# The second layer's modulation, from TensorE matmuls to sums over k tiles on VectorE

## The chip, the cores and the metric

One core of a Trainium2 chip runs the program. The metric is device time in microseconds (us) of one execution; the runs of the kernel before give a median of 1842.97 us (three runs, 1840.48 to 1843.57).

The engines are TensorE (PE in the profile; its weight loads are PEld), VectorE (DVE), ScalarE (ACT), GpSimd (POOL) and SyncE (SP), whose queue issues the DMAs.

## What is computed

The reference is a two-layer diffusion trunk over 512 latent and 256 context tokens of width 1024. Each layer scales and shifts its normed input by a modulation that depends on the conditioning vector alone:

```python
for l in range(DEPTH):                       # DEPTH = 2
    mod_l = (jax.nn.silu(c) @ ada_w[l] + ada_b[l])[:, None, :]     # ada_w[l]: 1024 x 6144
    mod_c = jax.nn.silu(c_ctx) @ ada_w[l] + ada_b[l]
    sh1, sc1, g1, sh2, sc2, g2 = jnp.split(mod_l, 6, axis=-1)
    csh1, csc1, cg1, csh2, csc2, cg2 = jnp.split(mod_c, 6, axis=-1)
    h_l = _rms(x, norm_w[l, 0]) * (1 + sc1) + sh1
    h_c = _rms(xc, norm_w[l, 0]) * (1 + csc1) + csh1
    ...
    x = x + g1 * (y_l @ w_o[l])
    x = x + g2 * _mlp(_rms(x, norm_w[l, 1]) * (1 + sc2) + sh2, mlp_w1[l], mlp_w2[l])
```

The MLP is `square(relu(h @ w1)) @ w2` with a hidden width of 4096. In the second layer the context is needed only as far as keys and values go, so of its modulation only the first third (shift and scale of the mixer's norm) is used.

## The kernel before

**Layout.** Features lie on the 128 partitions, tokens along the free dimension. A weight matrix is cut into chunks of 128 output columns; one chunk holds eight k tiles of 128x128. `linear` takes one chunk through PSUM: for the context's 256 columns and then for the latent's 512, eight k tiles by three passes (the numbers are split into a high and a low part, high x high, high x low, low x high), 24 matmuls each, into one bank, and then calls an evacuation. The tag `mm` has two banks, which alternate between context and latent.

**Weights.** `weight` loads a chunk in two pieces of 128x512 (tile `wst`, three buffers, L234), ScalarE casts the high part (`whi`, L250), GpSimd subtracts to get the low part (`wlo`, L251); six buffers each.

**The MLP** of the first layer (`mlp`) has four blocks b = 0..3; in each, eight up chunks and eight down chunks. The evacuation of an up chunk is a chain: ScalarE's relu into `tmp` (L1224), VectorE's product with PSUM (L1225), ScalarE's cast (L340), VectorE's subtraction (L341). That of a down chunk is one VectorE instruction that adds into the residual (L1240). The first three up chunks of b = 0 run together (`linears`), k tile by k tile, their matmuls at L289; all others run at L272.

**The modulation of the second layer** runs in the background of this MLP. It is a generator, `ada(rnd)` for rnd = 3, 4, 5, each for a third of the 6144 columns. For each of eight k tiles it loads two weight tiles of 128x1024 floats (tag `ast`, five buffers, L508), yields, and then has four matmuls (L512): the stationary operand is the 128x32 tile `cc[:, k]`, which holds the two conditioning vectors (latent, context) in its first two columns, the moving operand 512 columns of the weights, and each of the four writes another strip of 32 partitions of the bank `ad`, over the eight k tiles. Then `ada_out` transposes the bank on VectorE (L470) and adds the bias.

**Order.** `run` adds up the cost that each linear yields (its columns over 2400, 2.56 units for context and 5.12 for latent) and for each `pace` units takes one step of the background generator. Steps so stand in program order behind the evacuation of some linear. The program's engines get their instructions from a scheduler that simulates the program and prefers earlier ones in program order among those it thinks ready. Before block b = 3 what is left of the generator is run to its end.

```python
def tick(self, cost):
    self.clock += cost
    while self.clock >= self.pace:
        self.clock -= self.pace
        next(self.background, None)
```

Of the kernel before, what the change touches and what calls it, by code (L numbers as in the profile page):

```python
# [12 lines left out]
F32 = mybir.dt.float32  # L13
# [4 lines left out]
ALU = mybir.AluOpType  # L18
AX = mybir.AxisListType

P = 128
D = 1024
KT = 8
# [15 lines left out]

PACE = math.inf, 4.0
RATIO0, RATIO1, RATIO2 = 1.1, 1.6, 1.2
FILL0, FILL1 = 12, 6
NLAST, NFIRST = (2, 3), (3, 2)
# [10 lines left out]
def chain(*gens):  # L56
    for g in gens:
        yield from g
# [35 lines left out]
class Kernel:  # L94
    def __init__(self, ctx, tc, a):
# [8 lines left out]
        self.n, self.side = 0, 1  # L104
        self.clock, self.pace, self.background = 0.0, PACE[0], iter(())

# [59 lines left out]
    def mix(self, main, fill, ratio):  # L166

        done = [0.0, 0.0]
        gens = [iter(main), iter(fill)]
        while gens[0] is not None or gens[1] is not None:  # L170
            i = 0 if gens[1] is None or (gens[0] is not None and done[0] * ratio <= done[1]) else 1
            c = self.step(gens[i], i)
            if c is None:
                gens[i] = None
            else:
                done[i] += c
                yield c

    def weave(self, main, fill, ratio):
        self.run(self.mix(main, fill, ratio))  # L180
# [21 lines left out]
    def load(self, name, shape, dt=F32):  # L202
        t = self.cp.tile(list(shape), dt, tag=name, name=name)
        self.nc.sync.dma_start(t, self.a[name])
        return t

    def constants(self):
        nc, cp = self.nc, self.cp
        self.cmod = self.load("cmod", (P, 2, KT))
        self.ident = cp.tile([P, P], F32, tag="ident", name="ident")  # L210
        make_identity(nc, self.ident)
        self.ones = cp.tile([P, 32], F32, tag="ones", name="ones")
        nc.vector.memset(self.ones, 1.0)
        self.half = cp.tile([P, 32], F32, tag="half", name="half")
        nc.vector.memset(self.half, 0.0)
        nc.vector.memset(self.half[0:64, 0:16], 1.0)
        nc.vector.memset(self.half[64:128, 16:32], 1.0)
        self.adab = self.load("ada_b", (P, 2, 48))
        self.normw = self.load("norm_w", (P, 2, 2, KT))

# [242 lines left out]
        self.mod = [self.cp.tile([P, 48, 2], F32, tag=f"mod{l}", name=f"mod{l}") for l in range(2)]  # L463
        self.A = [[self.cp.tile([P, KT, 2], F32, tag=f"A{l}{n}", name=f"A{l}{n}") for n in range(2)] for l in range(2)]

    def ada_out(self, l, firsts, n, o):

        nc = self.nc
        tr = self.tmp()[:, :32 * n * len(firsts)]
        nc.vector.transpose(tr, o)  # L470
        for i, t0 in enumerate(firsts):
            mod = self.mod[l][:, t0:t0 + n, :]
            nc.vector.tensor_tensor(mod, tr[:, 32 * n * i:32 * n * (i + 1)].rearrange("p (t r) -> p t r", r=32)[:, :, 0:2],
                                    self.adab[:, l, t0:t0 + n].unsqueeze(2).to_broadcast([P, n, 2]), op=ALU.add)
            for m, first in enumerate((8, 32)):
                a, b = max(t0, first), min(t0 + n, first + 8)
                if a < b:
                    nc.vector.scalar_tensor_tensor(self.A[l][m][:, a - first:b - first, :], mod[:, a - t0:b - t0, :], 1.0,
                                                   self.normw[:, l, m, a - first:b - first].unsqueeze(2)
                                                   .to_broadcast([P, b - a, 2]), op0=ALU.add, op1=ALU.mult)  # L480
# [17 lines left out]
                yield 0.6  # L498
        self.ada_out(0, (2 * c, 8 + 2 * c), 2, o)

    def ada(self, rnd):

        nc = self.nc
        o = self.ps("ad")
        for k in range(KT):
            ws = [self.pieces() for _ in range(2)]
            for j, w in enumerate(ws):
                nc.sync.dma_start(w.rearrange("p a b -> p (a b)"), self.a["ada_w"][rnd - 1, k, j])  # L508
            yield 0.0
            for g in range(4):  # L510
                c = 32 * g
                nc.tensor.matmul(o[c:c + 32, :], lhsT=self.cc[:, k, :], rhs=ws[g // 2][:, g % 2, :], start=(k == 0),  # L512
                                 stop=(k == KT - 1), tile_position=(0, c))
            yield 1.0
        self.ada_out(rnd // 3, (rnd % 3 * 16,), 16, o)

    def ada_near(self):

# [750 lines left out]
    def main(self, out):  # L1269
        nc, a = self.nc, self.a  # L1270
# [4 lines left out]
        w = self.rows_weight(a["w_hv"])  # L1275
# [6 lines left out]
        acc = {}  # L1282
# [3 lines left out]
        r, f = self.norm_sums(acc, BOTH)  # L1286
# [71 lines left out]
        bc = self.proj_last(0, y2, x, BOTH)  # L1358
        first = self.mlp_first(0)
        h, ready = self.norm(x, self.A[0][1], self.mod[0][:, 24:32, :], bc)  # L1360
        self.clock, self.background, self.pace = 0.0, chain(*[self.ada(r) for r in range(3, 6)]), PACE[1]
        bc = self.mlp(0, h, x, BOTH, first, ready)

        w = self.rows_weight(a["w_dv"])
# [169 lines left out]
```

## Time and profile before

| | |
|---|---|
| median of three runs | 1842.97 us (1840.48 to 1843.57) |
| profiled execution | 1845.22 us, its span 1843.4 us |
| TensorE busy | 1765.9 us, 96% of the span |
| VectorE busy | 866.9 us, 47% |
| ScalarE busy | 756.3 us, 41% |
| GpSimd busy | 542.8 us, 29% |
| mean granted clock of TensorE | 0.991 of full |

The profile is one execution, recorded instruction by instruction. A row of a timeline gives the start from the beginning of the span, the duration (of several merged instructions from the first's start to the last's end), the engine, the line of the kernel, the operation, its output and inputs by their names in the program, their shapes and how many instructions are merged. In square brackets stands how long the engine was idle before, and what ended that. Matmuls are pipelined and overlap in the record, so the distance between two starts is what one costs, not its duration. A busy share is an average over stages; what bounds a stage is read from that stage.

### The profile page before, as it was taken

The page shows a single profiled execution, that of the slowest core. Times are in us where ns is not written, and L with a number is a line of the kernel's source. Part 1 is how long each engine was busy: PE and PEld are TensorE (multiplying, and loading weights), DVE is VectorE, ACT ScalarE, POOL GpSimd, SP SyncE. Part 2 cuts the span into 40 slices and gives each one's busy share as a digit, 9 for nine tenths or more (in the row PEclk, how much of TensorE's full clock was granted, in tenths as well). Part 3 has the DMA queues.
Part 4 walks back from the last instruction along what each step waited for, and adds up shares of the span by engine and source line. Part 5 has one row for each costly group of instructions (what it writes and reads, how often), then busy time and mean ns, then how long its engine had stood idle before and what let it go on. Part 6 is the DMA issues. An engine that isn't in the chain of part 4 may idle for free. (4 is left out here: it accounts for less than half of the span.)

```text
span 1843.4 us, 28900 instructions
## 1 busy us (share of the span) xinstructions
PE 1765.9 (96%) x11404; PEld 1447.1 (79%) x11404; DVE 866.9 (47%) x1964; ACT 756.3 (41%) x1510; POOL 542.8 (29%) x440
## 2 busy tenths in 40 slices
PE   5999999999999999999999999998998989999999
PEld 4877867787888877788888887776775878888887
DVE  5456766578555212211212237888769651212121
ACT  3554554466434212312312324566756343323241
POOL 0322323101122222223232321322233334444442
PEclk9999999999999999999999999999999989999999
DMA  8442241102133454412112131211121223233232
GB/s 304 139 137 77 98 150 42 38 24 98 46 103 133 154 171 165 141 60 64 63 63 63 63 98 63 67 41 35 41 88 57 75 69 97 97 98 97 97 98 92
DMA packets 81112, 170.94 MB, mean 93 GB/s; under 512 B 9424, under 2 KB 13008, under 8 KB 80976
## 3 DMA queue, kind: packets, MB, share of 16 engines
q1 hardware_dynamic: 80976, 169.09, 27.8%
q8 instruction: 89, 1.46, 0.3%
q14 instruction: 47, 0.39, 0.1%
HBM read 164.87 MB, written 4.19 MB: 92 GB/s over the span
## 5 line engine op out<-in xcount | busy, mean ns | idle before, releaser
L272 PE MATMUL mm<-lat,whi 128*128 128x512 f32 (+1 forms) x2908 | 908.8, 392 | 3.1 <-ACT tmpc L893 1.7
L251 POOL TENSOR_TENSOR wlo<-wst,whi 128x512 fp32r<-128x512 f32 (+1 forms) x374 | 484.9, 1298 | 1162.3 <-ACT whi L250 1080.7
L272 PEld LDWEIGHTS mm<-lat,whi 128*128 128x128 f32 x2908 | 535.2, 188 | 114.8 <-DVE tmpc L1225 5.1
L272 PE MATMUL mm<-lat,wlo 128*128 128x512 f32 (+1 forms) x1454 | 566.7, 390 | 0.0
L250 ACT CAST whi<-wst 128x512 fp32r<-128x512 f32 (+2 forms) x400 | 246.3, 618 | 686.1 <-PE mm L272 596.2
L272 PEld LDWEIGHTS mm<-lat,wlo 128*128 128x128 f32 x1454 | 273.6, 188 | 55.6 <-issue 0.4
L272 PE MATMUL mm<-ctx,whi 128*128 128x256 f32 x1604 | 306.3, 288 | 0.0
L272 PEld LDWEIGHTS mm<-ctx,whi 128*128 128x128 f32 x1604 | 256.6, 192 | 28.3 <-issue 13.7
L272 PE MATMUL mm<-ctx,wlo 128*128 128x256 f32 x802 | 229.0, 285 | 0.0
L1240 DVE SCALAR_TENSOR_TENSOR lat<-mm,mod,lat 128x512 f32<-128x512 f32 x64 | 48.0, 751 | 285.0 <-PE mm L272 285.0
L1225 DVE TENSOR_TENSOR tmp<-mm,tmp 128x512 f32<-128x512 f32 x61 | 42.1, 691 | 256.8 <-ACT tmp L1224 256.8
L272 PEld LDWEIGHTS mm<-ctx,wlo 128*128 128x128 f32 x802 | 154.2, 192 | 1.5 <-issue 1.0
L341 DVE TENSOR_TENSOR lat<-tmp,lat 128x512 fp32r<-128x512 f32 (+1 forms) x74 | 51.6, 700 | 41.0 <-ACT lat L340 40.7
L340 ACT CAST lat<-tmp 128x512 fp32r<-128x512 f32 (+1 forms) x74 | 45.8, 621 | 50.6 <-DVE tmp L1225 45.8
L817 PE MATMUL pv<-ast,lat 128*128 128x256 f32 x312 | 60.5, 302 | 2.4 <-ACT ast L340 1.7
L817 PEld LDWEIGHTS pv<-ast,lat 128*128 128x128 f32 x312 | 44.9, 189 | 12.0 <-ACT ast L340 8.7
L770 PE MATMUL sc<-lat,lat 128*128 128x512 f32 x144 | 45.9, 421 | 3.5 <-ACT p L788 2.4
L788 ACT ACTIVATE p<-ad,sm,sc 128x256 f32<-128x256 f32 x56 | 31.6, 564 | 30.2 <-DVE sm L781 30.0
L1240 DVE SCALAR_TENSOR_TENSOR ctx<-mm,mod,ctx 128x256 f32<-128x256 f32 x32 | 15.5, 483 | 58.8 <-PE mm L272 58.8
L340 ACT CAST ast<-tr 128x512 fp32r<-128x512 f32 x52 | 30.6, 589 | 28.8 <-PE tr L804 28.8
L341 DVE TENSOR_TENSOR ast<-tr,ast 128x512 fp32r<-128x512 f32 x52 | 35.6, 685 | 9.8 <-ACT ast L340 9.3
L804 PE MATMUL tr<-ident,p 128*128 128x128 f32 x208 | 33.7, 276 | 4.2 <-DVE p L1049 2.0
(399 smaller groups left out, 2105.5 us busy)
## 6 DMA issues: line engine op xcount, KB each, us to landing
wst<-in_mlp_w_dram SPq DMA_DIRECT2D x256, 256.0 KB, 2.6
ast<-in_ada_w_dram SPq DMA_DIRECT2D x83, 512.0 KB, 4.5
wst<-in_w_in_dram SPq DMA_DIRECT2D x76, 256.0 KB, 2.7
wst<-in_w_o_dram SPq DMA_DIRECT2D x32, 256.0 KB, 2.6
lat<-in_ada_w_dram SPq DMA_DIRECT2D x13, 512.0 KB, 9.0
lat<-in_x_dram SPq DMA_DIRECT2D x8, 512.0 KB, 6.3
ctx<-in_ctx_dram SPq DMA_DIRECT2D x8, 256.0 KB, 4.5
wst<-in_w_hv_dram SPq DMA_DIRECT2D x8, 256.0 KB, 8.5
```

The costliest lines, as they stand in the source:

```text
L250: nc.scalar.copy(hi[:, :w], st)
L251: (nc.gpsimd if n == P else nc.vector).tensor_sub(lo[:, :w], st, hi[:, :w].bitcast(F32))
L272: self.nc.tensor.matmul(o, lhsT=w(wp, k), rhs=xs[k].at(xp, s), start=(k == 0 and j == 0), stop=(k == nk - 1 and j == 2))
L340: self.nc.scalar.copy(hi, src)
L341: self.nc.vector.tensor_sub(lo, src, hi.bitcast(F32))
L770: nc.tensor.matmul(tiles[j][s], lhsT=l(qi, s), rhs=r(s), start=(i == 0), stop=(i == n - 1))
L788: nc.scalar.activation(p[j][s], tiles[j][s], AF.Exp, bias=neg[:, j:j + 1], scale=sc[:, j:j + 1], accum_out=sm[:, b, j:j + 1])
L804: self.nc.tensor.transpose(o[:, (2 * k + j) * P:(2 * k + j + 1) * P], p[j][s][:, (g + k) * P:(g + k + 1) * P], self.ident)
L817: self.nc.tensor.matmul(o, lhsT=v(x, k), rhs=pt[k][z], start=(k == 0 and j == 0), stop=(k == nk - 1 and j == 2))
L1225: nc.vector.tensor_mul(r, z, r)
L1240: nc.vector.scalar_tensor_tensor(x[m].at(s), z, self.mod[l][:, 40 + m, MOD[s]], x[m].at(s), op0=ALU.mult, op1=ALU.add)
```

## The change

`ada(rnd)` goes. A new generator, `ada_sums`, does the same three rounds on VectorE. A k tile's weights are multiplied by a column of `cc` (one vector's values for that k tile, one per partition) and added into accumulators of 128x512 floats, four for each vector (tag `p`). The first round does both vectors, the other two the latent's alone. What is left is a sum over partitions, for which four matmuls per vector with a constant stationary tile, `pick` (ones in column r), write the four strips of the bank `ad` as before; `ada_out` then runs as before.

The weight tiles are loaded one at a time, two ahead of their use. A step of the generator is one weight tile for one vector, two VectorE instructions. Five steps with loads alone come first; empty steps stand between the last sum, the matmuls and the transpose. The pace goes from 4.0 to 4.5 units a step. `keep_in_program_order` ties an instruction behind the one that the program wrote last on the same engine: an order of issue, without a semaphore.

```diff
--- before.py
+++ after.py
@@ -39,7 +39,7 @@
 
 
 
-PACE = math.inf, 4.0
+PACE = math.inf, 4.5
 RATIO0, RATIO1, RATIO2 = 1.1, 1.6, 1.2
 FILL0, FILL1 = 12, 6
 NLAST, NFIRST = (2, 3), (3, 2)
@@ -215,6 +215,11 @@
         nc.vector.memset(self.half, 0.0)
         nc.vector.memset(self.half[0:64, 0:16], 1.0)
         nc.vector.memset(self.half[64:128, 16:32], 1.0)
+
+        self.pick = cp.tile([P, 2, 32], F32, tag="pick", name="pick")
+        nc.vector.memset(self.pick, 0.0)
+        for r in range(2):
+            nc.vector.memset(self.pick[:, r, r:r + 1], 1.0)
         self.adab = self.load("ada_b", (P, 2, 48))
         self.normw = self.load("norm_w", (P, 2, 2, KT))
 
@@ -463,11 +468,11 @@
         self.mod = [self.cp.tile([P, 48, 2], F32, tag=f"mod{l}", name=f"mod{l}") for l in range(2)]
         self.A = [[self.cp.tile([P, KT, 2], F32, tag=f"A{l}{n}", name=f"A{l}{n}") for n in range(2)] for l in range(2)]
 
-    def ada_out(self, l, firsts, n, o):
+    def ada_out(self, l, firsts, n, o, pin=lambda ins: ins):
 
         nc = self.nc
         tr = self.tmp()[:, :32 * n * len(firsts)]
-        nc.vector.transpose(tr, o)
+        pin(nc.vector.transpose(tr, o))
         for i, t0 in enumerate(firsts):
             mod = self.mod[l][:, t0:t0 + n, :]
             nc.vector.tensor_tensor(mod, tr[:, 32 * n * i:32 * n * (i + 1)].rearrange("p (t r) -> p t r", r=32)[:, :, 0:2],
@@ -498,21 +503,51 @@
                 yield 0.6
         self.ada_out(0, (2 * c, 8 + 2 * c), 2, o)
 
-    def ada(self, rnd):
-
-        nc = self.nc
-        o = self.ps("ad")
-        for k in range(KT):
-            ws = [self.pieces() for _ in range(2)]
-            for j, w in enumerate(ws):
-                nc.sync.dma_start(w.rearrange("p a b -> p (a b)"), self.a["ada_w"][rnd - 1, k, j])
+    def ada_sums(self):
+
+
+
+        nc, pin = self.nc, self.tc.keep_in_program_order
+        src = [(rnd, k, j) for rnd in range(3, 6) for k in range(KT) for j in range(2)]
+        tiles = []
+
+        def load():
+            if src:
+                rnd, k, j = src.pop(0)
+                tiles.append(self.pieces())
+                nc.sync.dma_start(tiles[-1].rearrange("p a b -> p (a b)"), self.a["ada_w"][rnd - 1, k, j])
+
+        for n in range(5):
+            if n < 2:
+                load()
             yield 0.0
-            for g in range(4):
-                c = 32 * g
-                nc.tensor.matmul(o[c:c + 32, :], lhsT=self.cc[:, k, :], rhs=ws[g // 2][:, g % 2, :], start=(k == 0),
-                                 stop=(k == KT - 1), tile_position=(0, c))
-            yield 1.0
-        self.ada_out(rnd // 3, (rnd % 3 * 16,), 16, o)
+        for rnd in range(3, 6):
+            vecs = range(2 if rnd == 3 else 1)
+            acc = [[self.ptile() for _ in range(4)] for _ in vecs]
+            for k in range(KT):
+                for j in range(2):
+                    load()
+                    w = tiles.pop(0)
+                    for r in vecs:
+                        c = self.cc[:, k, r:r + 1]
+                        for g in range(2):
+                            t = acc[r][2 * j + g]
+                            if k == 0:
+                                pin(nc.vector.tensor_scalar(t, w[:, g, :], c, None, op0=ALU.mult))
+                            else:
+                                pin(nc.vector.scalar_tensor_tensor(t, w[:, g, :], c, t, op0=ALU.mult, op1=ALU.add))
+                        yield 0.0
+            yield 0.0
+            o = self.ps("ad")
+            for r in vecs:
+                for g in range(4):
+                    pin(nc.tensor.matmul(o[32 * g:32 * g + 32, :], lhsT=self.pick[:, r, :], rhs=acc[r][g], start=(r == 0),
+                                         stop=(r == len(vecs) - 1), tile_position=(0, 32 * g)))
+            del acc
+            yield 0.0
+            yield 0.0
+            self.ada_out(1, (rnd % 3 * 16,), 16, o, pin)
+            yield 0.0
 
     def ada_near(self):
 
@@ -1358,7 +1393,7 @@
         bc = self.proj_last(0, y2, x, BOTH)
         first = self.mlp_first(0)
         h, ready = self.norm(x, self.A[0][1], self.mod[0][:, 24:32, :], bc)
-        self.clock, self.background, self.pace = 0.0, chain(*[self.ada(r) for r in range(3, 6)]), PACE[1]
+        self.clock, self.background, self.pace = 0.0, self.ada_sums(), PACE[1]
         bc = self.mlp(0, h, x, BOTH, first, ready)
 
         w = self.rows_weight(a["w_dv"])
```

## Rows read from the trace of the kernel before

**Rows 1.** The page's busy times: us, share of the span, instructions, by engine

```profile
PE 1765.9 (96%) x11404; PEld 1447.1 (79%) x11404; DVE 866.9 (47%) x1964; ACT 756.3 (41%) x1510; POOL 542.8 (29%) x440
```

**Rows 2.** Busy us by stretch: PE, PEld, DVE, ACT, POOL; clock, DMA share, GB/s

```profile
574.00:800.00 226.00, 226.00 (x1326) 177.47 (x1325) 48.95 (x87) 58.12 (x107) 62.60 (x49) 1.00 0.47 158
...
800.00:1000.00 200.00, 200.00 (x1153) 177.01 (x1152) 38.14 (x66) 48.15 (x87) 61.95 (x49) 1.00 0.20 64
```

**Rows 3.** TensorE's groups of instructions by line, 560 to 810 us: busy, mean

```profile
L512 PE MATMUL ad<-ast,cc 128*32 128x512 f32 x192 | 25.8, 604 | 0.0
```

**Rows 4.** Timeline of TensorE between linears, 628 to 807 us: start, us, instruction

```profile
628.20 0.39 PE L272 MATMUL mm<-lat,wlo 128*128 128x512 f32 x1
628.42 0.40 PE L272 MATMUL mm<-ctx,whi 128*128 128x256 f32 x2
...
631.29 0.63 PE L272 MATMUL mm<-lat,whi 128*128 128x512 f32 x2
...
637.85 0.51 PE L272 MATMUL mm<-ctx,whi 128*128 128x256 f32 x2
...
647.38 0.51 PE L272 MATMUL mm<-ctx,whi 128*128 128x256 f32 x2
...
712.80 0.39 PE L272 MATMUL mm<-lat,wlo 128*128 128x512 f32 x1
...
798.84 0.40 PE L272 MATMUL mm<-ctx,whi 128*128 128x256 f32 x2
...
807.18 0.40 PE L272 MATMUL mm<-ctx,whi 128*128 128x256 f32 x2
```

**Rows 5.** Timeline behind the opening linear, 577 to 584 us: PE, PEld, DVE, POOL

```profile
577.98 0.39 PE L289 MATMUL sc<-lat,wlo 128*128 128x512 f32 x1
...
580.15 0.51 PE L272 MATMUL mm<-ctx,whi 128*128 128x256 f32 x2
...
583.64 0.14 PEld L512 LDWEIGHTS ad<-ast,cc 128*32 128x32 f32 x4 [0.27 <-DMA ast<-in_ada_w_dram]
...
577.97 1.29 DVE L1225 TENSOR_TENSOR tmp<-mm,tmp 128x512 f32<-128x512 f32 x2 [3.76 <-ACT tmp L1224]
...
579.48 1.96 DVE L341 TENSOR_TENSOR lat<-tmp,lat 128x512 fp32r<-128x512 f32 x2 [0.23 <-ACT lat L340]
...
581.05 1.55 POOL L251 TENSOR_TENSOR wlo<-wst,whi 128x512 fp32r<-128x512 f32 x1 [0.76 <-ACT whi L250]
```

**Rows 6.** Instructions of three VectorE lines: duration ns min/median/max, first and last start

```profile
L421 DVE SCALAR_TENSOR_TENSOR tmp<-lat,A,tmp x8: 742/744/747, 27.1 to 57.1; 128x512 f32<-128x512 f32 x8
...
L423 DVE SCALAR_TENSOR_TENSOR lat<-tmp,mod,lat x24: 737/744/1779, 28.8 to 1136.6; 128x512 fp32r<-128x512 f32 x24
...
L619 DVE TENSOR_SCALAR lat<-lat,oml x8: 474/475/480, 77.9 to 235.2; 128x512 f32<-128x512 f32 x8
```

**Rows 7.** Timeline of VectorE, a down evacuation and an up weight's two chains

```profile
646.50 0.75 DVE L1240 SCALAR_TENSOR_TENSOR lat<-mm,mod,lat 128x512 f32<-128x512 f32 x1 [4.98 <-PE mm L272]
...
708.18 0.43 DVE L1225 TENSOR_TENSOR tmpc<-mm,tmpc 128x256 f32<-128x256 f32 x1 [3.73 <-ACT tmpc L1224]
709.08 0.42 DVE L341 TENSOR_TENSOR ctx<-tmpc,ctx 128x256 fp32r<-128x256 f32 x1 [0.47 <-ACT ctx L340]
714.19 0.69 DVE L1225 TENSOR_TENSOR tmp<-mm,tmp 128x512 f32<-128x512 f32 x1 [4.69 <-ACT tmp L1224]
...
715.57 0.69 DVE L341 TENSOR_TENSOR lat<-tmp,lat 128x512 fp32r<-128x512 f32 x1
```

**Rows 8.** SP's queue, 647 to 665 us; the page's DMA issues (median to landing)

```profile
647.48 0.80 SPq L508 DMA_DIRECT2D ast<-in_ada_w_dram  x2
...
657.91 7.09 SPq L234 DMA_DIRECT2D wst<-in_mlp_w_dram  x2
...
ast<-in_ada_w_dram SPq DMA_DIRECT2D x83, 512.0 KB, 4.5
```

**Rows 9.** Timeline of VectorE in the opening

```profile
2.58 0.25 DVE L462 TENSOR_TENSOR cc<-cmod,sm 128x8 f32<-128x8 f32 x2 [1.23 <-ACT sm L458]
```

## The prediction

> **What bounds the kernel now.** I read the page's busy shares first: TensorE is busy for 1765.9 us of a span of 1843.4, VectorE for 866.9 [rows 1]. An average says nothing of one stage, so the next view is the table by stretch. From 574 to 800 us, where the first layer's MLP runs together with the modulation of the second layer, TensorE is busy in 226.00 of 226 us; from 800 to 1000 us, where no modulation is left, in 200.00 of 200 [rows 2]. VectorE is busy for 48.95 us in the first stretch, a fifth of it [rows 2]. So in this stage the end is set by what stands in TensorE's queue, and the matmuls of L512 stand in it: 192 records, whose time not shared with others is 25.8 us by the groups of lines [rows 3]. The loop issues 96 matmuls there, so each is two records, and the timeline shows them in 24 groups of four matmuls, eight records.
>
> **What the removed matmuls cost.** The timeline of TensorE gives the price as the distance between starts. A weight's two linears, context and latent, take 9.53 us with a group behind them (637.85 to 647.38) and 8.34 without (798.84 to 807.18): 1.19 us a group [rows 4]. I price 21 groups so, 25.0 us. The other three are at the start. Two stand together behind the opening three-weight linear: 577.98 to 580.15, less the 0.22 that lies between linears without a group (628.20 to 628.42), 1.95 us [rows 4, 5]. One waited 0.27 us for its second tile [rows 5]: 1.46. Sum removed: 28.4 us, all of it on the path, since TensorE does not idle.
>
> **What is added on TensorE.** Sixteen matmuls of the same shape (32 columns, 512 wide, 4-byte): eight in a row for the first of the three rounds, which sums for two vectors, four for each of the other two. By the prices above 1.95 + 1.19 + 1.19 = 4.3 us. They wait for VectorE's sums, but the generator leaves an empty step between the last sum and them. There are 5 + 36 + 20 + 20 = 81 steps, one for every 4.5 units of cost, and the three blocks hold 48 weights of 7.68 units, 368.64; counted out, each set of matmuls comes at least one whole linear behind the one after which its last sum stands. So I cost the wait at nothing; its cover is that linear, 2.87 us or more (628.42 to 631.29 [rows 4]).
>
> **What was hidden under the removed groups.** At 578 us the latent outputs of the opening linear end nearly together, and the next linear needs the first of their banks. VectorE's two products run from 577.97 for 1.29 us, so the first bank is free at about 578.6 and the second at 579.3 [rows 5]. The two groups covered that. Without them TensorE could go on at 578.20 and stands until about 578.7: I give back 0.5 us (0 if the bank is free earlier, 1.1 if the second one counts). The rest of VectorE's backlog there meets none of the new sums, since the generator's first five steps hold loads alone and use up the opening linear's ticks.
>
> **What is added on VectorE.** 128 instructions over 128x512 floats: 16 products with a column, and 112 products with a sum in place. Nearest rows: a product with a column, SBUF to SBUF, 475 ns at the median; a product and product with both tensors in SBUF, 744; another such line 737 to 1779 [rows 6]. That is 16 x 0.475 + 112 x 0.744 = 91 us; the upper end, with 1.78 for all of the 112, is 207, the lower 90. I take 744, the row of the same operands and shape, and keep 1.78 for a rival.
>
> Where it lies: a step holds two instructions (1.5 us); a weight has 7.68 / 4.5 = 1.71 steps, 2.54 us in 8.34. In the up half of a block the context chain takes VectorE 1.32 us (708.18 to 709.50) and the latent one 2.07 (714.19 to 716.26), waits for ScalarE included [rows 7]: 3.4, with the steps 5.9 of 8.34. In the down half an evacuation is one instruction, 0.75 us for latent [rows 7] and less for context: 4.0 at most. Behind a tied instruction the next evacuation is queued, and for that TensorE waits. The tightest place is the latent evacuation of the up half: VectorE's product ends at 714.88 [rows 7]; the last matmul before it started at 712.80, and with 0.22 to the context linear and its 2.87 us [rows 4] the bank is needed again at 715.9. So 1.0 us is to spare. In front of that product stand the steps of the context tick, one at most (a remainder under 4.5, and 2.56, make less than two steps): the chain to 709.50, the step to 711.0, 3.2 us before the product starts. Two steps come only behind a latent linear: 3.0 us behind a chain that ends 2.8 us after its linear let the context product start some 6 us after it, and that bank is needed at 8.3. So by order alone nothing stalls and the 91 us cost nothing. If the cover goes, an up weight loses what chains and steps have above 8.34 us.
>
> The Trainium skill speaks against this instruction: "Vector Engine (DVE) Microarchitecture Reference", section "Points that are easy to get wrong", has a scalar_tensor_tensor with two SBUF sources that are not bf16 at half throughput. This trace disagrees: with both in SBUF the median is 744 ns [rows 6], with one in PSUM 0.75 us [rows 7]. By the rule the time would be that of rival B at twice the price.
>
> GpSimd does collide with VectorE. At 579.48 two subtractions took 1.96 us where one takes 0.69 elsewhere, and GpSimd's at 581.05 took 1.55 us [rows 5, 7]. GpSimd runs twice for each weight; were each VectorE instruction that it meets held for those 1.55 us, a weight would lose 3.1 and come to 9.0 of 8.34, with half of that 7.5. GpSimd itself prepares a weight some two weights ahead (six buffers, two a weight), so its own delay has over 10 us of cover.
>
> **What moves.** The modulation's weight tiles go one at a time, two ahead of their use: the same 48 tiles of 512 KB, 4.5 us from issue to landing [rows 8], and two tiles are two steps or more, 9 units or 9.8 us at 8.34 us for 7.68 units. They pass through SP's queue with the linears' weights, two of which stood there for 7.09 us where two issues take 0.80 [rows 8]: rival C's place. Three small memsets join the opening, ahead of a VectorE instruction that waits 1.23 us [rows 9]; even at 0.4 us each they fit in: nothing.
>
> **Sum.** 28.4 - 4.3 - 0.5 = 23.6 us. Against the profiled execution (1845.22 us, its span 1843.4) that is 1821.6. The median of the runs shown, 1842.97, is 2.25 us below it, and the forecast is made for the median: 1819.4. What follows the MLP moves forward as it is; its order may come out slightly otherwise, as the program is ordered anew, and I allow 2 us for that.
>
> **Rivals.**
>
> A, the forecast: 1819.4, own range 1817 to 1822. For it: TensorE without idle time, and linears at 8.34 us a weight where no group covers anything.
>
> B, the added instructions are held so long that the up half's VectorE work no longer fits. At twice the price, 1.49 us, a weight needs 3.4 + 5.1 = 8.5, 0.16 over, on 21 up weights 3 us: 1823. At 1.78 it is 9.5, 1.14 over, 24 us: 1843, no change. Between them 3 to 12 us lost, 1822 to 1831, are the likelier part. For it: 1.78 has been seen [rows 6]. Against it: GpSimd is busy for 62.60 of 226 us [rows 2], so most instructions meet nothing. The Trainium skill's page "SBUF — State Buffer", section "SBUF: two separate sides", says that VectorE with two SBUF inputs and GpSimd shut each other out for a whole instruction; the 1.96 us fit that.
>
> C, slower: a tied instruction stands at the head of VectorE's queue for a tile that SP has not fetched, the evacuations behind it, and TensorE behind these. In the last two rounds, 32 tiles, each wait beyond the spare 1.0 us is TensorE's. The gain is gone at 23.6 / 32 = 0.74 us of stall, a wait of 1.7 us for each tile; from 1.9 it is slower by a measurable amount; a wait of 2.5 gives 1819 + 32 x 1.5 = 1867. For it: 7.09 - 0.80 = 6.3 us in SP's queue and 4.5 of landing make 10.8 against 9.8 us of lead, 1 us late in the bad case. Against it: five buffers let the loads run further ahead than the two tiles written, and the one wait for a tile in the trace is 0.27 us [rows 5].
>
> D, the change does not do what it says: the ties set an order of issue, but a sum still lands ahead of an evacuation, or the new order is worse elsewhere, and the gain is lost: within 0.2%, about 1842.
>
> **How the numbers follow.** A 0.81, B up to 12 us lost 0.09, B's far end and D 0.05, C 0.05. The range takes in A, the part of B up to some 7 us lost, and on the lower side A's own end less 1.5 us, the 0.5 not given back and 1 us should eight matmuls in a row cost what four do: 1815.5 to 1826. A measurement of this kernel can tell about 0.2%, 3.7 us, from no change. Faster by more: A and the nearer B, 0.90; within: 0.05; slower: 0.05.
>
> **What would show it.** Right: 8.34 us a weight throughout the MLP's first three blocks with TensorE busy in all of it; L512's records gone and 32 of the new kind there; VectorE's new groups of 16 and 112 with means near 0.48 and 0.75 to 0.95 us; a stop of half a microsecond behind the opening linear. Wrong: up weights above 8.4 us, TensorE's idle time ended by VectorE's products (B), VectorE's idle time ended by loads of the modulation's weights (C), or a shorter MLP and longer stages behind it (D).

## The result

The first set of executions gave 1814.78 us (median of four, 1814.54 to 1821.37) against 1842.64 for before: a ratio of 0.9852, 95% interval 0.9836 to 0.9867, faster by 27.9 us. The forecast was 1819.4 with a range of 1815.5 to 1826: the direction was right, and the time lies 0.7 us below the range. Three later sets of the same kernel lay 25.2, 25.5 and 25.2 us below before, with medians inside the range (experiment 1).

The profiled execution of after took 1821.37 us, its span 1819.6. The page's busy times:

```profile
PE 1741.8 (96%) x11244; PEld 1445.9 (79%) x11244; DVE 969.8 (53%) x2095; ACT 755.9 (42%) x1510; POOL 545.7 (30%) x440
```

Against [rows 1] TensorE has 24.1 us and 160 records less (192 of the old kind gone, 32 of the new there), VectorE 102.9 us more. Between the two profiled executions the spans differ by 23.8 us. The tables by stretch show where. The stretch runs from just before the last latent product of the MLP's norm to the first context product of the next layer's norm; first line before, second after (columns as in [rows 2]):

```profile
569.00:1117.00 548.00, 547.60 (x3172) 461.14 (x3170) 127.88 (x226) 146.45 (x267) 158.37 (x123) 1.00 0.32 106
```

```profile
568.60:1092.80 524.20, 523.35 (x3011) 458.50 (x3009) 232.02 (x355) 146.25 (x267) 158.86 (x123) 1.00 0.36 110
```

The stretch is 23.8 us shorter, TensorE is busy in all of it but 0.85 us, and VectorE goes from 127.88 to 232.02 us in it. VectorE's norm instructions bound the stages (first and last start of each group; before, then after):

```profile
L421 DVE SCALAR_TENSOR_TENSOR tmp<-lat,A,tr x8: 733/734/747, 558.6 to 569.2; 128x512 f32<-128x512 f32 x8
L421 DVE SCALAR_TENSOR_TENSOR tmpc<-ctx,A,mm x8: 440/474/475, 1117.1 to 1123.4; 128x256 f32<-128x256 f32 x8
```

```profile
L426 DVE SCALAR_TENSOR_TENSOR tmp<-lat,A,tr x8: 741/742/748, 558.0 to 568.6; 128x512 f32<-128x512 f32 x8
L426 DVE SCALAR_TENSOR_TENSOR tmpc<-ctx,A,mm x8: 439/472/474, 1092.8 to 1099.1; 128x256 f32<-128x256 f32 x8
```

The MLP's latent product starts at 558.6 before and 558.0 after, the next norm at 1117.1 and 1092.8. I call what lies between them the MLP stage: 558.5 us before, 534.8 after. Outside it the two traces show the same order of instructions on ScalarE, GpSimd and SyncE; VectorE has three more memsets in the opening, and on TensorE a few neighbouring matmuls of the first layer's attention change places.

TensorE between linears, after (timeline; answers to [rows 4, 5]):

```profile
577.44 0.39 PE L294 MATMUL sc<-lat,wlo 128*128 128x512 f32 x1
578.18 0.50 PE L277 MATMUL mm<-ctx,whi 128*128 128x256 f32 x2 [0.35 <-DVE tmp L1260]
...
695.03 0.40 PE L277 MATMUL mm<-ctx,whi 128*128 128x256 f32 x2
703.37 0.40 PE L277 MATMUL mm<-ctx,whi 128*128 128x256 f32 x2
...
744.84 0.39 PE L277 MATMUL mm<-lat,wlo 128*128 128x512 f32 x1
745.16 1.92 PE L544 MATMUL ad<-p,pick 128*32 128x512 f32 x16
747.01 0.51 PE L277 MATMUL mm<-ctx,whi 128*128 128x256 f32 x2
...
846.97 0.39 PE L277 MATMUL mm<-lat,wlo 128*128 128x512 f32 x1
847.29 1.06 PE L544 MATMUL ad<-p,pick 128*32 128x512 f32 x8
848.29 0.51 PE L277 MATMUL mm<-ctx,whi 128*128 128x256 f32 x2
```

A weight takes 8.34 us (695.03 to 703.37), as forecast. The new matmuls stand between linears, as the old ones did; the two sets shown take 2.17 and 1.32 us between starts. Behind the opening linear the next start comes after 0.74 us in place of the usual 0.22.

VectorE in an up and in a down stretch, after (timeline; answers to [rows 7]), GpSimd's subtraction in the second of them, and VectorE's sums (duration min/median/max):

```profile
697.57 0.69 DVE L346 TENSOR_TENSOR lat<-tmp,lat 128x512 fp32r<-128x512 f32 x1 [0.69 <-ACT lat L345]
698.18 2.74 DVE L538 SCALAR_TENSOR_TENSOR p<-ast,cc,p 128x512 f32<-128x512 f32 x4
700.83 0.42 DVE L1260 TENSOR_TENSOR tmpc<-mm,tmpc 128x256 f32<-128x256 f32 x1
...
645.19 0.75 DVE L1275 SCALAR_TENSOR_TENSOR lat<-mm,mod,lat 128x512 f32<-128x512 f32 x1 [3.60 <-PE mm L277]
645.86 2.36 DVE L538 SCALAR_TENSOR_TENSOR p<-ast,cc,p 128x512 f32<-128x512 f32 x2
648.13 0.47 DVE L1275 SCALAR_TENSOR_TENSOR ctx<-mm,mod,ctx 128x256 f32<-128x256 f32 x1
648.53 1.40 DVE L538 SCALAR_TENSOR_TENSOR p<-ast,cc,p 128x512 f32<-128x512 f32 x2
```

```profile
645.70 1.30 POOL L256 TENSOR_TENSOR wlo<-wst,whi 128x512 fp32r<-128x512 f32 x1 [1.43 <-ACT whi L255]
```

```profile
L538 DVE SCALAR_TENSOR_TENSOR p<-ast,cc,p x112: 735/746/1801, 606.4 to 936.0; 128x512 f32<-128x512 f32 x112
```

Each sum stands right behind an evacuation, as the tie has it. At 698.18 there are two steps behind a latent evacuation, four instructions, and the context product behind them still starts at 700.83. The pair at 645.86 begins while GpSimd's subtraction runs and takes 2.36 us, the one at 648.53 meets none and takes 1.40. The group's mean is 960 ns, its busy time 102.6 us (neighbours overlap a little in the record).

### The profile page after: what moved, and what is told of

Read it like the earlier page. It is cut to its first block, busy times and chain, and to the rows that moved or that the text cites. A ratio compares the mean times of both kernels' runs of the same rounds, so it can differ in the third digit from the quotient of the medians.

```text
span 1819.6 us, 28719 instructions
## 1 busy us (share of the span) xinstructions
PE 1741.8 (96%) x11244; PEld 1445.9 (79%) x11244; DVE 969.8 (53%) x2095; ACT 755.9 (42%) x1510; POOL 545.7 (30%) x440
## 5 line engine op out<-in xcount | busy, mean ns | idle before, releaser
L538 DVE SCALAR_TENSOR_TENSOR p<-ast,cc,p 128x512 f32<-128x512 f32 x112 | 102.6, 960 | 0.0
```

Source lines behind the costliest of these rows:

```text
L538: pin(nc.vector.scalar_tensor_tensor(t, w[:, g, :], c, t, op0=ALU.mult, op1=ALU.add))
```

## Experiments

**1. The same two kernels again.** `e1_after_again`, `e8_after_third` and `e10_after_fourth` are the changed kernel, `e2_before_again` the one before, all without an edit.

> The changed kernel once more, unchanged. The profiles of before and after put 23.8 us of gain into the first layer's MLP, the first forecast's sum was 23.6; the medians differ by 27.9. Theory 1 (the gain is TensorE's matmuls and nothing else; the other 4 us are scatter of the stages outside the MLP between executions): the difference of the medians of many executions falls to 22 to 26 us, a ratio of 0.986 to 0.988, and the MLP, from the first down evacuation to the last, is as long here as in the first profile within 0.5 us. Theory 2 (the change also makes stages outside the MLP shorter, as a rule): the difference stays at 27 to 29, ratio 0.985 or less, and the profile shows a stage outside the MLP that is shorter than before's by some 4 us.

> The kernel before once more, as a kernel of its own, beside the shared runs of before. Both theories: ratio 1.000 with an interval of 0.002 or less. Theory 1: the executions scatter by 3 to 7 us by the mean granted clock, and the profile of this one shows stages outside the MLP that differ from the first profile's by some us at the same program. Theory 2: executions within 3 us of each other, stages alike within 1 us.

> The changed kernel a third time, for the 3 us that its executions so far (median of eight 1816.7) lie below what the MLP stage's 23.8 us explain (1843.2 less 23.8 is 1819.4). Theory 1 (scatter by the granted clock in stages outside the MLP, in which the order of instructions is the same in both kernels): executions between 1814 and 1822 again, their median 1816 to 1820, stages outside the MLP different by 1 to 4 us between profiles of this one kernel. Theory 2 (the later start in time puts the clock's drops at better places, as a rule): median 1815 to 1817.5 again.

> The changed kernel a fourth time, for its distance to before. Theory 1 (25.2 and 25.5 us in the two later sets are its distance, 27.9 in the first one was scatter): 24 to 26.5 us below before. Theory 2: 27 or more.

Measured: e1 1817.99 (before beside it 1843.17), ratio 0.9863 (0.9851 to 0.9876); e8 1818.28 (1843.75), 0.9866 (0.9849 to 0.9882); e10 1818.74 (1843.95), 0.9863 (0.9849 to 0.9876). e2 1843.89, ratio 0.9999 (0.9989 to 1.0008), its twelve executions from 1839.87 to 1848.27. So the bands of theory 1 for the distance (22 to 26, then 24 to 26.5 us) and for e8's median held, and the 27.9 of the first set did not come back. The MLP stage is 534.7, 534.8 and 534.7 us in their profiles and 558.4 in e2's. What differs between profiles of one and the same program lies outside it. The stage of the second layer's attention, after and e1 (columns as in [rows 2]):

```profile
1101.00:1454.90 353.90, 326.06 (x1734) 253.18 (x1732) 281.16 (x665) 200.69 (x414) 103.44 (x89) 0.98 0.18 58
```

```profile
1100.80:1451.70 350.90, 324.01 (x1733) 250.30 (x1731) 280.74 (x665) 200.53 (x414) 103.93 (x89) 0.99 0.18 58
```

and the norm ahead of the MLP stage, again after and e1:

```profile
548.80:558.00 9.20, 7.88 (x57) 7.55 (x58) 8.03 (x28) 4.30 (x9) 0.72 (x1) 0.81 0.10 32
```

```profile
548.30:556.20 7.90, 6.60 (x58) 6.22 (x59) 7.90 (x28) 4.30 (x9) 0.71 (x1) 1.00 0.11 37
```

The mean granted clock of this norm is 0.81 in one execution and 1.00 in another, and the norm is 9.2 or 7.9 us long; the attention stage is some 3 us longer at 0.98 than at 0.99. Where the norm took 9.2 us, TensorE was busy for 1.32 of 3 us from 548 to 551, and from 551.5 to 554.5 its clock stood at 0.50, the lower of its two levels (1.2 GHz):

```profile
548.00:551.00 3.00, 1.32 (x13) 0.77 (x13) 3.00 (x8) 1.60 (x4) 1.27 (x1) 1.00 0.32 102
551.50:554.50 3.00, 3.00 (x16) 3.00 (x15) 3.00 (x13) 1.43 (x3) 0.00 (x0) 0.50 0.03 10
```

The MLP stage, in which TensorE hardly stops, stands at 1.00 in all of them. The four profiles of after differ ahead of this norm (547.4 to 550.1 us), in it (7.9 or 9.2), in the norm behind the MLP (8.3 or 9.9) and in the attention (350.9 to 353.8); what follows takes 364.7 us in each. In all, the profiles have 1280.6 to 1284.8 us outside the MLP stage, those of before 1284.9 and 1285.8.

The mean granted clock of every execution is on record too: the three executions that make the first median (1814.54 to 1814.99 us) ran at 0.993 or 0.994, the profiled one beside them (1821.37) at 0.990, and all twelve of the three later sets at 0.992. A thousandth of 1815 us is 1.8 us, so by an estimate that counts the whole of it as TensorE's time the first median would lie 1.8 to 3.6 us below the later ones; it lies 3.2 to 4.0 below. That the clock alone did it is not shown: e1's executions at 0.992 lie between 1815.49 and 1821.10 us.

Theory 1 of e2 gave a scatter of 3 to 7 us and stages that differ by some us. The scatter was 8.4; the stages of its profile are those of the first profile of before within 1 us, as its theory 2 had it.

**2. The matmuls alone.** `e3_one_k_tile` is the kernel before with the modulation's matmuls for the first k tile only (the other seven k tiles are left out of the sum):

```diff
-            for g in range(4):
+            for g in range(4 if k == 0 else 0):
                 c = 32 * g
-                nc.tensor.matmul(o[c:c + 32, :], lhsT=self.cc[:, k, :], rhs=ws[g // 2][:, g % 2, :], start=(k == 0),
-                                 stop=(k == KT - 1), tile_position=(0, c))
+                nc.tensor.matmul(o[c:c + 32, :], lhsT=self.cc[:, k, :], rhs=ws[g // 2][:, g % 2, :], start=True,
+                                 stop=True, tile_position=(0, c))
```

`e6_matmuls_back` is the changed kernel with the matmuls put back, their result unused; `e11_half_back` does it for every second k tile (`range(4 if k % 2 else 0)`):

```diff
+                z = self.ps("ad")
+                for g in range(4):
+                    pin(nc.tensor.matmul(z[32 * g:32 * g + 32, :], lhsT=self.cc[:, k, :], rhs=self.cos, start=True,
+                                         stop=True, tile_position=(0, 32 * g)))
```

> The kernel before with the modulation's matmuls for the first k tile alone: the other seven k tiles are loaded but left out of the sum, so 21 of 24 groups of four go and no VectorE work comes. Theory 1: the groups cost 1.19 us each on TensorE, so 21 groups or some 25 us less, with 0.5 given back at the opening linear: 24 to 25 us below before, and level with the changed kernel within 1.5 us, which has four groups in place of three and all of the VectorE work: that work is free. If the VectorE work cost something (rival B), this kernel would lie below the changed one by that amount, 3 us or more.

> The changed kernel with a group of four matmuls put back for every k tile, 24 groups, of the old shape, into the bank that is free, their result unused; the sums on VectorE stay. Theory 1: TensorE's price comes back whole, 24 x 1.19 = 28.6 us above the changed kernel, 28 to 30, and level with before plus 4 us less the scatter. If part of the gain came from elsewhere in the change (the order of loads, the tile pace), less than 28.6 comes back: under 26.

> The changed kernel with a group of four matmuls put back for every second k tile, 12 groups. Theory 1: 12 x 1.2 = 14.4 us more in the MLP stage than the changed kernel's 534.7, 549 to 550, whatever the other stages do; the median 13 to 16 us above the changed kernel's, since the start of the later stages lies halfway between the two kernels. Theory 2 (the stages outside the MLP depend on when they start): the median off from the MLP stage's share by more than 2 us.

Measured: e3 1817.16 us, ratio 0.9859 (0.9846 to 0.9872), 26.0 below before where 24 to 25 were expected, and 0.8 below e1; its MLP stage 533.3 us, 25.2 below before's 558.5. e6 1848.87, ratio 1.0032 (1.0020 to 1.0044), its MLP stage 563.5, 28.8 above e1's 534.7. e11 1836.58, ratio 0.9956 (0.9943 to 0.9968), its MLP stage 549.1, 14.4 above e10's 534.7. The rows that bound these stages, e3, e6, e11:

```profile
L421 DVE SCALAR_TENSOR_TENSOR tmp<-lat,A,tr x8: 735/738/748, 557.4 to 568.0; 128x512 f32<-128x512 f32 x8
L421 DVE SCALAR_TENSOR_TENSOR tmpc<-ctx,A,mm x8: 437/472/475, 1090.7 to 1097.0; 128x256 f32<-128x256 f32 x8
```

```profile
L426 DVE SCALAR_TENSOR_TENSOR tmp<-lat,A,tr x8: 737/738/749, 558.9 to 569.5; 128x512 f32<-128x512 f32 x8
L426 DVE SCALAR_TENSOR_TENSOR tmpc<-ctx,A,mm x8: 440/472/475, 1122.4 to 1128.7; 128x256 f32<-128x256 f32 x8
```

```profile
L426 DVE SCALAR_TENSOR_TENSOR tmp<-lat,A,tr x8: 743/746/749, 557.8 to 568.4; 128x512 f32<-128x512 f32 x8
L426 DVE SCALAR_TENSOR_TENSOR tmpc<-ctx,A,mm x8: 440/480/487, 1106.9 to 1113.3; 128x256 f32<-128x256 f32 x8
```

So 24 groups cost 28.8 us in the stage and 12 cost 14.4: 1.20 us a group each time, with all the sums on VectorE beside them. e3 has three groups and no sums, the changed kernel four groups' worth and all the sums; e3's stage is 1.4 us shorter than e1's. By the prices of the prediction the added sets cost 4.3 us and e3's three groups 3.6, and the stop of 0.5 us behind the opening linear is absent from e3, where a group stands in that place: 1.2 us. What is left for the sums on VectorE is 0.2 us or so. The group of e3 behind the opening linear, with no idle time before it:

```profile
577.14 1.06 PE L512 MATMUL ad<-ast,cc 128*32 128x512 f32 x8
```

The medians do not follow the stage as closely: e6 lies 30.9 above e1 (28 to 30 were expected), e11 17.8 above e10 (13 to 16 were expected), where the stage gives 28.8 and 14.4. The second of these is off by more than the 2 us that theory 2 named. Taken as median less MLP stage, the rest of the program is 1283 to 1284 us in e1, e8 and e10 (1280 in the first set of after), 1284 to 1286 in the sets of before, 1285 in e6 and 1287 in e11. The profiles of e6 and e11 themselves have 1284.4 and 1283.7 us outside the stage, no more than those of before and after, so no trace shows a later stage that became longer. Whether the 2 to 3 us are scatter or a matter of when the later stages start isn't settled.

**3. Without the ties.** `e4_untied` takes all ties off; `e9_tie_first` takes them off the 112 products with a sum and keeps them on the first k tile's 16 products, the matmuls and the transposes:

```diff
-        nc, pin = self.nc, self.tc.keep_in_program_order
+        nc, pin = self.nc, lambda ins: ins
```

```diff
-                                pin(nc.vector.scalar_tensor_tensor(t, w[:, g, :], c, t, op0=ALU.mult, op1=ALU.add))
+                                nc.vector.scalar_tensor_tensor(t, w[:, g, :], c, t, op0=ALU.mult, op1=ALU.add)
```

> The changed kernel without the ties: the same sums on VectorE, their place in its queue left to the schedule's own model. Theory 1 (what the tie buys is that no sum stands ahead of an evacuation for which TensorE waits): sums float ahead and wait for weight tiles or hold evacuations; TensorE gets idle time in the MLP ended by VectorE's products, and of the 23.8 us some 3 to 20 are lost. Theory 3 (the ties do nothing, the schedule's order is as good): the time is within 1.5 us of the changed kernel's, the MLP stage within 0.5 us.

> The changed kernel with the ties kept on the first k tile's 16 products, the matmuls and the transposes, and taken off the 112 products with a sum. Untied altogether, the sums began at 517.6 us, before the MLP, and cost 9.5 us there and 15.5 in the MLP. Theory 4 (what hurts is to stand ahead of the MLP's norm and wait for tiles there): with the first products held in place nothing floats ahead of the MLP, the stage before it is as short as in the changed kernel, and of the 25 us at most 5 come back: MLP stage 535 to 540. Theory 5 (sums in a row hurt wherever they stand, since the schedule's model puts them into VectorE's gaps by durations that are too short): the MLP stage is longer by 8 us or more, with TensorE's idle time ended by VectorE's products.

Measured: e4 1845.67, ratio 1.0011 (1.0001 to 1.0020): the whole gain is gone, more than the 3 to 20 us that were expected. Its first products begin at 517.58, long before the MLP, behind a wait for a weight tile:

```profile
517.58 0.88 DVE L536 TENSOR_SCALAR p<-ast,cc 128x512 f32<-128x512 f32 x2 [2.03 <-DMA ast<-in_ada_w_dram]
```

Ahead of the MLP and where it begins the tables say (columns as in [rows 2]):

```profile
524.00:550.00 26.00, 25.27 (x147) 21.19 (x146) 26.00 (x44) 8.81 (x17) 7.02 (x5) 1.00 0.54 169
550.00:575.00 25.00, 19.01 (x112) 16.68 (x112) 22.34 (x56) 10.26 (x21) 3.08 (x2) 0.80 0.21 65
```

VectorE is busy for 26.00 of 26 us ahead of the MLP; behind that TensorE stops, and its mean granted clock is 0.80 from 550 to 575 us. The part of the program ahead of the MLP's norm is 10 us longer than in other profiles (the norm's first context product at 559.4 against 547.4 to 550.8), the MLP stage, 550.2 us, 15.5 longer than after's.

e9 1842.44, ratio 0.9993 (0.9984 to 1.0002). Nothing floats ahead of the MLP here (first sum at 590.9), and yet the MLP stage is 557.6 us, 22.9 longer than after's. Theory 4 falls. Theory 5 stands as far as its result goes; the reason that it gives, durations in the schedule's model that are too short, no run tests. From 600 to 640 us, one of TensorE's stops in it, VectorE ahead of that stop, and TensorE's waits in the whole MLP stage (us in total, times, longest):

```profile
600.00:640.00 40.00, 35.04 (x198) 30.41 (x197) 39.97 (x56) 10.52 (x21) 15.14 (x8) 1.00 0.55 162
```

```profile
630.31 0.73 PE L277 MATMUL mm<-lat,whi 128*128 128x512 f32 x2 [1.97 <-DVE tmp L1260]
```

```profile
622.86 6.79 DVE L538 SCALAR_TENSOR_TENSOR p<-ast,cc,p 128x512 f32<-128x512 f32 x7
629.58 0.68 DVE L1260 TENSOR_TENSOR tmp<-mm,tmp 128x512 f32<-128x512 f32 x1
```

```profile
PE mm L277 <- DVE tmp L1260: 10.0, 7, 2.9
PE mm L277 <- DVE lat L1275: 5.2, 2, 2.7
```

The untied sums stand in rows that fill VectorE for 39.97 of 40 us: seven in a row, 6.79 us, ahead of the product at 629.58, and the latent linear that needs this product's bank begins when TensorE has stood idle for 1.97 us. The waits for VectorE's products and evacuations come to 15.2 us in the stage. TensorE's mean granted clock, 1.00 throughout after's MLP stage, is 0.94 here from 640 to 700 us, 0.98 from 760 to 830 and 0.99 from 830 to 900; by an estimate from these rows (60 x 0.06 + 70 x 0.02 + 70 x 0.01) that is 5.7 us more of the 22.9. The same 128 instructions, tied, lie one or two steps at a time behind an evacuation, and TensorE hardly stops.

**4. How much room VectorE has.** `e5_twice` does each product a second time into an unused tile, `e7_pace4` sets the pace back to 4.0:

```diff
+                            pin(nc.vector.scalar_tensor_tensor(scr, w[:, g, :], c, t, op0=ALU.mult, op1=ALU.add))
```

```diff
-PACE = math.inf, 4.5
+PACE = math.inf, 4.0
```

> The changed kernel with every one of the 112 products with a sum done twice, the second time into an unused tile: VectorE's added work doubles to some 210 us (0.96 us each, as the first profile has them). Theory 1 with the account of rival B: an up weight then needs 3.4 + 1.71 x 4 x 0.96 = 10.0 us of VectorE in 8.34, so each of the 21 up weights that has steps loses some 1.6 us, 30 us or so in all (15 to 40), with TensorE's idle time ended by VectorE's products; the down weights, 1.2 + 6.6 = 7.8 us, lose nothing. If VectorE's work is hidden altogether (queue depth, banks): under 3 us. If VectorE's work already cost something in the changed kernel: more than 40.

> The changed kernel at the pace of before, 4.0 units a step instead of 4.5: VectorE gets 1.92 steps a weight instead of 1.71 and is done earlier. Theory 1: an up weight's VectorE work is 3.4 + 3.7 = 7.1 of 8.34 us, still hidden: within 1.5 us of the changed kernel. If VectorE were at its edge (rival B): 2 us or more above it.

Measured: e7 1819.65, ratio 0.9870 (0.9855 to 0.9885), its MLP stage 534.7: no difference there, so VectorE is not at its edge and the pace as such does nothing to the stage; the median is 1.4 us above e8's, within the 1.5 that theory 1 allowed. e5 (128 instructions more, as the first products are doubled too) 1831.85, ratio 0.9940 (0.9925 to 0.9955), its MLP stage 546.4: 11.6 us lost, where 15 to 40 were expected. The waits of TensorE in its MLP stage (us in total, times, longest):

```profile
PE mm L277 <- DVE tmp L1262: 8.1, 9, 1.6
PE mm L277 <- DVE lat L1277: 1.4, 1, 1.4
```

and VectorE's own inside the chains, first after, then e5:

```profile
DVE lat L346 <- ACT lat L345: 20.8, 31, 0.7
DVE ctx L346 <- ACT ctx L345: 13.6, 29, 0.5
```

```profile
DVE lat L346 <- ACT lat L345: 20.8, 31, 0.7
...
DVE ctx L346 <- ACT ctx L345: 6.5, 14, 0.5
```

The account was wrong in size. It counted the chain at 3.4 us, waits for ScalarE included, and a loss on each of 21 up weights. Of the waits inside the chains the context's fall by half in e5 (13.6 us in 29 become 6.5 in 14), the latent's stay as they are (20.8 in 31); and TensorE stops at ten places in all, not on each up weight. With none of the waits (0.42 + 0.43 + 0.69 + 0.69 = 2.2 us) and 1.71 steps of four at 0.96 (6.6) an up weight would need 8.8 us, 0.5 over, on 21 weights 10, near the 11.6 measured; but that is worked out afterwards, and the latent's waits are still there, so the agreement does not show the cause. What sets the 11.6 us stays open.

## Why the prediction was right or wrong

**What bounds the stage, and the price of a group: right.** 1.19 us were read from the distance between starts, 1.20 came of putting 24 and 12 groups back.

**The sum: right.** 23.6 us were forecast. The MLP stage got shorter by 23.7 to 23.8 us in four profiles. The added matmuls cost 1.95 us at 744.84 (2.17 less 0.22), as forecast, and 1.10 at 846.97, where the pair of matmuls behind them is slower than others (0.51 against 0.40 us), against 1.19; the stop behind the opening linear is 0.35 us by its own row and 0.5 by the starts, against 0.5.

**VectorE's price: between the bounds, and hidden.** 744 ns were taken for one, the median is 746, the mean 960, just above the 0.75 to 0.95 us given as a sign, for GpSimd holds 26 of them up; 102.6 us in place of 83 for the 112. Little or nothing of that reached TensorE (0.2 us or so by e3), so rival B did not come. The Trainium skill's rule of half throughput ("Vector Engine (DVE) Microarchitecture Reference", "Points that are easy to get wrong") would have doubled it; the median of 746 speaks against it, as the row of before did.

**Rival C did not come:** no wait of the sums for a tile shows among VectorE's waits in the MLP stage of after, while untied products did wait for tiles (2.03 us at 517.58 in e4).

**Rival D did not come, and e4 and e9 show what it would have cost.** The tied sums stand behind the evacuations as the change says, and the order elsewhere stayed; without the ties nothing of the gain is left. The prediction put this at the time of before, about 1842 us; e9 took 1842.44 and e4 1845.67.

**What was wrong: the range.** The step that failed is the one from the sum to the median of the runs. It carried one profiled execution's distance to its own median (2.25 us) over to the changed kernel, let what follows the MLP move forward "as it is", and allowed 2 us for that. After's profiled execution took 1821.37 us, 0.2 from the 1821.6 that the sum gives, but it lies 6.6 us above the median of its set. Outside the MLP one program's executions differ by several us: 1280.6 to 1284.8 us in four profiles of after, with the mean granted clock of stages in which TensorE pauses; the twelve executions of e2 span 8.4 us. So the medians of four executions each lie between 1814.78 and 1818.74 us, and a term of plus or minus 3 us for that belonged in the range; the executions of before known by then, 1840.48 to 1845.22 us, already lay 4.7 us apart. The first set was some 2.6 us further below before than the three later ones (27.9 against 25.2 to 25.5); its three low executions had a higher mean granted clock than all of the later sets (0.993 or 0.994 against 0.992), and why they had it stays open. So does why even the later sets lie 1.4 to 1.7 us beyond the 23.8 of the stage: in the profiles the rest of the program is shorter after than before by 0.1 to 5.2 us, which scatter of this size can give.

## What to carry to other kernels

Where one engine is busy all the time in a stage, work taken off its queue is worth its price between starts, and what it hid there (here 0.5 us at one place) must be subtracted. Moving it to an engine with room is only half of the change: that engine also lets banks go, so in this kernel each moved instruction had to stand right behind an evacuation, a step or two at a time; the same instructions in rows cost as much as the move gained. And before a range is given, look at how far executions of the unchanged kernel lie apart.

## What was not expected of the hardware

A product with a sum over 128x512 floats took 1.40 us a pair when GpSimd was idle and 2.36 beside one of its 1.30 us subtractions. Of the 112, 26 began while such a subtraction ran; each of them ended 0.55 us after the subtraction and took 1.69 to 1.80 us, the other 86 took 735 to 749 ns. GpSimd lost nothing by it: its subtractions kept their mean, 1301 against 1298 ns. The norm ahead of the MLP ran at a mean granted clock of 0.81 or 1.00 in two executions of one program, 9.2 or 7.9 us.

```profile
L256 POOL TENSOR_TENSOR wlo<-wst,whi 128x512 fp32r<-128x512 f32 x122 | 158.7, 1301 | 360.2 <-ACT whi L255 360.2
```
